# Order of the weight units in the feature-major products of an encoder trunk

## The chip, the cores and the metric

One core of one Trainium2 chip runs the whole program in one launch. The metric is device time in microseconds (us): the median of three runs of the kernel before is 2489.68 us (2489.42 to 2490.61).

## The reference

Two encoder layers over 256 tokens of width 2048, in float32. Layer 0 mixes with dilated-window attention (8 heads, three groups) and differential attention (4 heads), layer 1 with grouped-query attention (8 heads) and neighbourhood attention (8 heads). Every layer ends in a gated feed-forward part (FFN) of width 5632. Cut to what matters here:

```python
def conv_ffn(x, w_up, conv_w, conv_b, w_down):
    h = jnp.einsum("bsd,df->bsf", x, w_up)
    g, u = h[..., :D_FF], h[..., D_FF:]
    gp = jnp.pad(g, ((0, 0), (1, 1), (0, 0)))
    g = conv_w[0] * gp[:, :-2] + conv_w[1] * gp[:, 1:-1] + conv_w[2] * gp[:, 2:] + conv_b
    return jnp.einsum("bsf,fd->bsd", jax.nn.gelu(g) * u, w_down)

def reference(x, ...):
    for layer in range(DEPTH):
        y = rmsnorm(h, ln_mix[layer])
        mix = even_mixer(y, ...) if layer % 2 == 0 else odd_mixer(y, ...)
        h = h + mix
        h = h + conv_ffn(rmsnorm(h, ln_ffn[layer]), ...)
    return rmsnorm(h, ln_final)
```

Nearly all the arithmetic is products of the 256 token rows with weight matrices: the input projections of the attention, their output projections, the FFN's up (gate and value) and down.

## The kernel before, in words

**Precision.** Each float32 operand is split into a high part that TensorE takes as it is and a low part, the rest. A product is high times high, plus high times low, plus low times high, all summed in PSUM. For weights the high part `wh` is a cast by ScalarE (ACT, `split`, line 191) and the low part `wl` a subtraction by VectorE (DVE, line 192); each covers one unit of 128 x 1024 weights (`wunit`), which a DMA on the SP queue has brought. There are four buffers each for `wh` and `wl`, so a cast waits until TensorE has finished with the unit four before.

**Two kinds of product.** Token-major products (`gemm_a`, lines 152 to 154) have tokens on the output's partitions and only 512-column matmuls; they serve the FFN's down part, the output projections and some value projections. Feature-major products (`gemm_b`) have features on the output's partitions: they serve the queries and keys (48 + 16 + 16 of them) and the FFN's gate and value (176). One `gemm_b` sums over 2048 in two units of eight 128-blocks each. In `b_unit` each block has a 512-column matmul (line 124: `wh` times the activation's high and low parts side by side, 256 columns each) and a 256-column one (line 127: `wl` times the activation's high part, added onto the second half of the same PSUM bank). Per unit the eight of line 124 come first, then the eight of line 127. So a chain of `gemm_b` calls is eight wide, eight narrow, eight wide, eight narrow, and so on.

**Around it.** The result `gm` (four PSUM buffers) is taken out by `halves`: ACT copies the first half (line 181), DVE adds the second (line 182) and multiplies by the row factor (line 187). The small products of attention (transposes into `tp`, scores and values into `s`) are issued between two large products by a list of due times (`later`, `tick`, `flush`). A scheduler then puts each engine's instructions in order, by when it expects operands to be ready; where the first gate and value products of an FFN wait for the last transposed activations `yT`, it mixes their matmuls with the transposes (line 233).

Of the kernel before, what the change touches and what calls it, by code (L numbers as in the profile page):

```python
# [35 lines left out]
KT = D // P  # L36
# [21 lines left out]
def trunk_kernel(ctx: ExitStack, tc, a, out):  # L58
    nc = tc.nc
    V, S, G, T = nc.vector, nc.scalar, nc.gpsimd, nc.tensor  # L60
# [11 lines left out]
    def nm(s):  # L72
        uid[0] += 1
        return f"{s}_{uid[0]}"
# [27 lines left out]
    def tps(tag, bufs):  # L102
        return psum.tile([P, 512], F32, name=nm(tag), tag=tag, bufs=bufs)

    def wunit(src, parts=1):
        raw = wts.tile([P, UN], F32, name=nm("raw"), tag="raw", bufs=RAW)
        nc.sync.dma_start(raw, src)
        wh = wts.tile([P, UN], F32R, name=nm("wh"), tag="wh", bufs=4)
        wl = wts.tile([P, UN], F32R, name=nm("wl"), tag="wl", bufs=4)
        for i in range(parts):  # L110
            sl = slice(i * UN // parts, (i + 1) * UN // parts)
            split(wh[:, sl], wl[:, sl], raw[:, sl])
        return wh, wl

    def two(ap):
        return ap.rearrange("p (a b) -> p a b", a=2)

    def b_unit(ps, src, u, act):
        wh, wl = wunit(src[u])
        flat = ps.rearrange("p a b -> p (a b)")  # L120
        cols = [slice(k * P, (k + 1) * P) for k in range(8)]
        for k, sl in enumerate(cols):
            y = act[u * 8 + k]
            T.matmul(flat, wh[:, sl], y.rearrange("p a b -> p (a b)"), start=(u == 0 and k == 0), stop=False)  # L124
        for k, sl in enumerate(cols):
            y = act[u * 8 + k]
            T.matmul(ps[:, 1, :], wl[:, sl], y[:, 0, :], start=False, stop=(u * 8 + k == KT - 1))  # L127

    def gemm_b(src, act):

        ps = two(tps("gm", 4))
        for u in range(2):
            b_unit(ps, src, u, act)
        tick()
        return ps
# [20 lines left out]
    def gemm_a(src, act, nk, strided=False, hooks={}, first=1):  # L156

        ps = [tps("gm", 4), tps("gm", 4)]
        for u in range(nk // 2):
            if u in hooks:  # L160
                hooks[u]()
            a_unit(ps, src, u, act, nk, strided, parts=1 if u else first)
            if u % 2 == 1:
                tick()
        return ps
# [123 lines left out]
    def qk_tile(src, act, r, order, slot):  # L289
        t = halves(gemm_b(src, act), r, order)  # L290
        y = new_qk("qk", slot)
        split(y[:, 0, :], y[:, 1, :], t)
        return y
# [94 lines left out]
    ps = two(tps("tp", 2))  # L388
# [7 lines left out]
    ps = tps("s", 2)  # L396
# [4 lines left out]
    ps = tps("s", 2)  # L401
# [87 lines left out]
    for hh in range(2):  # L489
        vg = []  # L490
        for g in range(3):
            ps = v_ps.pop(0) if v_ps else gemm_a(a["eva_v"][hh * 3 + g], yT, KT, strided=(g > 0))
# [77 lines left out]
    for pair in range(2):  # L570
        vt = v_tiles(gemm_a(a["evb_v"][pair], yT, KT), rstd, range(20 - 4 * pair, 24 - 4 * pair))
        for hd in (2 * pair, 2 * pair + 1):
# [4 lines left out]
            for m in range(2):  # L577
                q = qk_tile(a["evb_qk"][hd * 4 + m], yT, Rq, rev, 2 * m)
                k = qk_tile(a["evb_qk"][hd * 4 + 2 + m], yT, R, None, 2 * m + 1)
# [5 lines left out]
    def ffn(layer, yT, gain, last=False):  # L585
        R = None
        res = None
        for half in range(2):
            prod = []
            for i in range(HALF_F):  # L590
                f = half * HALF_F + i
                if f == 0:
                    pg, pu = two(tps("gm", 4)), two(tps("gm", 4))
                    b_unit(pg, a["up"][layer, f, 0], 0, yT)
                    b_unit(pu, a["up"][layer, f, 1], 0, yT)
                    flush()
                    R = row_broadcast(row_factor())
                    b_unit(pg, a["up"][layer, f, 0], 1, yT)
                    b_unit(pu, a["up"][layer, f, 1], 1, yT)
                else:  # L600
                    pg = gemm_b(a["up"][layer, f, 0], yT)
                g = halves(pg, R)
                c = tmp.tile([P, SEQ], F32, name=nm("cv"), tag="cv")
                V.tensor_scalar(c, g, convw[:, layer, 1, f:f + 1], convb[:, layer, f:f + 1],
                                op0=ALU.mult, op1=ALU.add)
                V.scalar_tensor_tensor(c[:, 1:SEQ], g[:, 0:SEQ - 1], convw[:, layer, 0, f:f + 1],
                                       c[:, 1:SEQ], op0=ALU.mult, op1=ALU.add)
                V.scalar_tensor_tensor(c[:, 0:SEQ - 1], g[:, 1:SEQ], convw[:, layer, 2, f:f + 1],
                                       c[:, 0:SEQ - 1], op0=ALU.mult, op1=ALU.add)
                S.activation(c, c, AF.Gelu_apprx_tanh)  # L610
                if f:
                    pu = gemm_b(a["up"][layer, f, 1], yT)
                u = halves(pu, R)
                V.tensor_tensor(c, c, u, op=ALU.mult)
                y = new_act("prod", f % NACT)
                split(y[:, 0, :], y[:, 1, :], c)
                prod.append(y)
# [89 lines left out]
    ps = gemm_a(a["odc"][0], yT, KT, hooks={6: flush})  # L707
# [10 lines left out]
    for n in range(2):  # L718
        ps = gemm_a(a["odc"][1 + n], yT, KT)
# [6 lines left out]
    for hh in range(2):  # L726
        vt = v_tiles(gemm_a(a["od_v"][hh], yT, KT), rstd, ((18, 19, 20, 21), (16, 17, 22, 23))[hh])
        for hd in range(hh * 4, hh * 4 + 4):
            y = att.tile([P, 6, 64], F32, name=nm("nb"), tag="bias", bufs=2)
# [6 lines left out]
            k = qk_tile(a["od_qk"][hd * 2 + 1], yT, R, None, hd % 2 * 2 + 1)  # L736
# [157 lines left out]
```

## Time and profile before

| | |
|---|---|
| median of three runs | 2489.68 us |
| the profiled execution | 2489.95 us |
| its span, first to last instruction | 2488.2 us |
| TensorE (PE) busy | 99% of the span |
| weight loads (PEld) busy | 85% |
| VectorE (DVE) busy | 67% |
| ScalarE (ACT) busy | 49% |
| mean granted TensorE clock | 0.999 |

Rows of the timeline merge instructions of a kind that follow each other (x8). A matmul's duration in them is that of one matmul from its start to a modelled end, and consecutive matmuls overlap; what one costs in a chain is read from start to start.

### The profile page before, as it was taken

Reading aid. Unit: us, or ns where it says so; the run is one execution under the profiler, and the core shown is the slowest. Engines: PE = TensorE matmul, PEld = TensorE weight load, DVE = VectorE, ACT = ScalarE, POOL = GpSimd, SP = SyncE. Lnnn points to the kernel's source line nnn. Section 1 sums busy time; section 2 is a strip of 40 time slices with the busy share of each in tenths; the row PEclk is TensorE's granted clock in tenths of the full one; section 3 lists DMA queues with packets and bytes.
Section 4 is the critical chain, followed back from the end, with each engine's and each line's share of the span. In section 5 each row is a group of like instructions: output and inputs, shape, how many; then the busy total and the mean of one; then the engine's idle time right before and its main releaser. Section 6 shows DMA issues by size and latency. Waiting matters only on the chain.

```text
span 2488.2 us, 34307 instructions
## 1 busy us (share of the span) xinstructions
PE 2470.9 (99%) x13106; PEld 2122.7 (85%) x13106; DVE 1671.2 (67%) x2461; ACT 1227.6 (49%) x1853; POOL 35.9 (1%) x68
## 2 busy tenths in 40 slices
PE   8999999999999999999999999999999999999998
PEld 7888888888888888888888888888888888888887
DVE  5676577676577775577775568765777755777754
ACT  6454445465554443344444457545544443444443
POOL 1000000000000000000000000000000000000000
PEclk9999999999999999999999999999999999999999
DMA  8655555555555555555555555765555555555554
GB/s 296 197 175 176 185 178 179 173 176 156 187 189 190 187 188 192 195 188 190 190 186 187 187 185 170 173 176 178 187 188 190 189 187 194 194 187 188 191 189 144
DMA packets 129749, 463.86 MB, mean 186 GB/s; under 512 B 15188, under 2 KB 15220, under 8 KB 129584
## 3 DMA queue, kind: packets, MB, share of 16 engines
q1 hardware_dynamic: 126800, 455.17, 53.2%
q0 software_dynamic: 2784, 6.50, 2.4%
q8 instruction: 102, 1.67, 0.3%
q14 instruction: 63, 0.52, 0.1%
HBM read 459.44 MB, written 2.17 MB: 186 GB/s over the span
## 4 chain that ended last, share of the span: by engine, by line
PE 75%; DMA 0%; DVE 0%; ACT 0%; issue 0%; DVEq 0%; ACTq 0%
PE gm L124 28%; PE gm L127 15%; PE gm L153 10%; PE gm L152 10%; PE gm L154 10%; PE tp L233 0%; PE tp L326 0%; DMA nb<-in_rpb 0%; PE s L338 0%; PE s L337 0%; PE s L311 0%; PE s L309 0%; PE s L336 0%; PE s L310 0%; PE tp L668 0%; DVE wl L192 0%
## 5 line engine op out<-in xcount | busy, mean ns | idle before, releaser
L192 DVE TENSOR_TENSOR wl<-raw,wh 128x1024 fp32r<-128x1024 f32 (+1 forms) x857 | 1047.4, 1223 | 705.1 <-ACT wh L191 702.3
L191 ACT CAST wh<-raw 128x1024 fp32r<-128x1024 f32 (+1 forms) x857 | 898.7, 1049 | 1141.3 <-issue 498.7
L124 PE MATMUL gm<-yT,wh 128*128 128x512 f32 x4096 | 1029.1, 393 | 0.0
L124 PEld LDWEIGHTS gm<-yT,wh 128*128 128x128 f32 x4096 | 736.6, 189 | 132.5 <-DVE yT L196 0.7
L127 PEld LDWEIGHTS gm<-yT,wl 128*128 128x128 f32 x4096 | 558.7, 190 | 39.8
L127 PE MATMUL gm<-yT,wl 128*128 128x256 f32 x4096 | 571.2, 282 | 0.0
L152 PE MATMUL gm<-wh,prod 128*128 128x512 f32 x704 | 274.5, 390 | 0.0
L154 PE MATMUL gm<-wh,prod 128*128 128x512 f32 x704 | 274.3, 390 | 0.0
L153 PE MATMUL gm<-wl,prod 128*128 128x512 f32 x704 | 274.0, 389 | 0.0
L152 PE MATMUL gm<-wh,yT 128*128 128x512 f32 x416 | 164.9, 396 | 6.6 <-ACT wh L191 6.6
L153 PE MATMUL gm<-wl,yT 128*128 128x512 f32 x416 | 163.9, 394 | 0.3 <-DVE wl L192 0.3
L154 PE MATMUL gm<-wh,yT 128*128 128x512 f32 x416 | 163.5, 393 | 0.0
L154 PEld LDWEIGHTS gm<-wh,prod 128*128 128x128 f32 x704 | 132.2, 188 | 27.4
L152 PEld LDWEIGHTS gm<-wh,prod 128*128 128x128 f32 x704 | 132.2, 188 | 27.1
L153 PEld LDWEIGHTS gm<-wl,prod 128*128 128x128 f32 x704 | 132.2, 188 | 27.1
L182 DVE TENSOR_TENSOR t<-t,gm 128x256 f32<-128x256 f32 x256 | 105.9, 414 | 0.0
L153 PE MATMUL gm<-wl,mix 128*128 128x512 f32 x256 | 100.5, 393 | 1.1 <-DVE wl L192 1.1
L152 PE MATMUL gm<-wh,mix 128*128 128x512 f32 x256 | 101.0, 395 | 0.0
L154 PE MATMUL gm<-wh,mix 128*128 128x512 f32 x256 | 100.3, 393 | 0.0
L152 PEld LDWEIGHTS gm<-wh,yT 128*128 128x128 f32 x416 | 79.2, 190 | 22.7 <-ACT wh L191 6.6
L153 PEld LDWEIGHTS gm<-wl,yT 128*128 128x128 f32 x416 | 79.3, 191 | 17.0 <-DVE wl L192 1.6
L154 PEld LDWEIGHTS gm<-wh,yT 128*128 128x128 f32 x416 | 79.1, 190 | 16.5
(206 smaller groups left out, 1506.4 us busy)
## 6 DMA issues: line engine op xcount, KB each, us to landing
raw<-in_up SPq DMA_DIRECT2D x352, 512.0 KB, 3.3
raw<-in_down SPq DMA_DIRECT2D x176, 512.0 KB, 3.2
raw<-in_eva_qk SPq DMA_DIRECT2D x96, 512.0 KB, 3.2
raw<-in_eva_v SPq DMA_DIRECT2D x48, 512.0 KB, 3.7
raw<-in_evb_qk SPq DMA_DIRECT2D x32, 512.0 KB, 3.3
raw<-in_ev_out SPq DMA_DIRECT2D x32, 512.0 KB, 3.5
raw<-in_od_qk SPq DMA_DIRECT2D x32, 512.0 KB, 3.3
raw<-in_od_out SPq DMA_DIRECT2D x32, 512.0 KB, 3.3
```

Source lines behind the costliest of these rows:

```text
L124: T.matmul(flat, wh[:, sl], y.rearrange("p a b -> p (a b)"), start=(u == 0 and k == 0), stop=False)
L127: T.matmul(ps[:, 1, :], wl[:, sl], y[:, 0, :], start=False, stop=(u * 8 + k == KT - 1))
L152: T.matmul(ps[t], ah, wh[:, sl], start=(kt == 0), stop=False)
L153: T.matmul(ps[t], ah, wl[:, sl], start=False, stop=False)
L154: T.matmul(ps[t], al, wh[:, sl], start=False, stop=(kt == nk - 1))
L182: V.tensor_tensor(t0, t0, ps[:, 1, :], op=ALU.add)
L191: S.copy(dst_h, src)
L192: V.tensor_tensor(dst_l, src, dst_h.bitcast(F32), op=ALU.subtract)
```

## The change

In `b_unit` the first unit (u = 0) keeps its order, and the second unit issues its eight 256-column matmuls ahead of its eight 512-column ones. The flag that closes the sum moves from the last narrow matmul to the last wide one. Number, shape and operands of the matmuls stay the same. Lines behind the edit stand three lower in the changed file; there the wide matmul is line 127 and the narrow one line 130.

```diff
--- before.py
+++ after.py
@@ -119,12 +119,15 @@
         wh, wl = wunit(src[u])
         flat = ps.rearrange("p a b -> p (a b)")
         cols = [slice(k * P, (k + 1) * P) for k in range(8)]
-        for k, sl in enumerate(cols):
+        high = [(True, k, sl) for k, sl in enumerate(cols)]
+        low = [(False, k, sl) for k, sl in enumerate(cols)]
+        for hi, k, sl in high + low if u == 0 else low + high:
             y = act[u * 8 + k]
-            T.matmul(flat, wh[:, sl], y.rearrange("p a b -> p (a b)"), start=(u == 0 and k == 0), stop=False)
-        for k, sl in enumerate(cols):
-            y = act[u * 8 + k]
-            T.matmul(ps[:, 1, :], wl[:, sl], y[:, 0, :], start=False, stop=(u * 8 + k == KT - 1))
+            if hi:
+                T.matmul(flat, wh[:, sl], y.rearrange("p a b -> p (a b)"), start=(u == 0 and k == 0),
+                         stop=(u * 8 + k == KT - 1))
+            else:
+                T.matmul(ps[:, 1, :], wl[:, sl], y[:, 0, :], start=False, stop=False)
 
     def gemm_b(src, act):
```

On TensorE, in a gate product in mid FFN (`gm_7013`; `wh_7016` and `wl_7017` are its first unit's weights, `wh_7038` and `wl_7039` its second's, `gm_7068` the product behind it), the order before is:

```order
L127 MATMUL gm_7013<-yT_6139,wl_7017 128x256
L124 MATMUL gm_7013<-yT_6297,wh_7038 128x512 [waits Activation_49]
L124 MATMUL gm_7013<-yT_6302,wh_7038 128x512
...
L124 MATMUL gm_7013<-yT_6495,wh_7038 128x512
L127 MATMUL gm_7013<-yT_6297,wl_7039 128x256 [waits DVE_49]
...
L127 MATMUL gm_7013<-yT_6495,wl_7039 128x256
L124 MATMUL gm_7068<-yT_6101,wh_7071 128x512 [waits Activation_49]
L124 MATMUL gm_7068<-yT_6106,wh_7071 128x512
```

In the change the same place on TensorE reads:

```order
L130 MATMUL gm_7013<-yT_6139,wl_7017 128x256
L130 MATMUL gm_7013<-yT_6297,wl_7039 128x256 [waits DVE_49]
L130 MATMUL gm_7013<-yT_6302,wl_7039 128x256
...
L130 MATMUL gm_7013<-yT_6495,wl_7039 128x256
L127 MATMUL gm_7013<-yT_6297,wh_7038 128x512 [waits Activation_49]
...
L127 MATMUL gm_7013<-yT_6495,wh_7038 128x512
L127 MATMUL gm_7068<-yT_6101,wh_7071 128x512 [waits Activation_49]
L127 MATMUL gm_7068<-yT_6106,wh_7071 128x512
```

The eight narrow rows of the second unit now stand right behind those of the first, and its eight wide rows right ahead of those of the next product. The wait for `wl_7039` (a DVE result) comes eight wide matmuls earlier than before.

On ACT, in the same part (casts `wh` of coming units, the copy `t` out of the products `gm_7013` and `gm_7068`, the GELU `cv`), the order before is:

```order
L181 COPY t_1376_7058<-gm_7013 128x256 [waits PE_49]
L191 CAST wh_7180<-raw_7178 128x1024 [waits DMAHW7_49,PE_49,Activation_49]
L191 CAST wh_7202<-raw_7200 128x1024 [waits DMAHW0_49,PE_49,Activation_49]
L610 ACTIVATE cv_7063<-cv_7063 128x256 [waits DVE_49]
L181 COPY t_1386_7113<-gm_7068 128x256 [waits PE_49]
L191 CAST wh_7234<-raw_7232 128x1024 [waits DMAHW1_49,PE_49,Activation_49]
L191 CAST prod_7119<-cv_7063 128x256 [waits DVE_49]
L191 CAST wh_7256<-raw_7254 128x1024 [waits DMAHW2_49,PE_49,Activation_49]
```

In the change the same place on ACT reads:

```order
L184 COPY t_1376_7058<-gm_7013 128x256 [waits PE_49]
L194 CAST wh_7147<-raw_7145 128x1024 [waits DMAHW6_49,Activation_49]
L194 CAST wh_7180<-raw_7178 128x1024 [waits DMAHW7_49,PE_49,Activation_49]
L613 ACTIVATE cv_7063<-cv_7063 128x256 [waits DVE_49]
L184 COPY t_1386_7113<-gm_7068 128x256 [waits PE_49]
L194 CAST wh_7202<-raw_7200 128x1024 [waits DMAHW0_49,Activation_49]
L194 CAST prod_7119<-cv_7063 128x256 [waits DVE_49]
L194 CAST wh_7234<-raw_7232 128x1024 [waits DMAHW1_49,PE_49,Activation_49]
```

The cast of `wh_7202`, which waits for a second unit's buffer, has moved behind the GELU and the copy out of `gm_7068`.

On TensorE at the first FFN's start (transposes `tp` of the last activations; `gm_6430` the first gate, `gm_6431` the first value product, `gm_6577` the next gate), ahead of the second-last pair of transposes, the order before is:

```order
L233 MATMUL tp_6487<-ident,h 128x128 [waits PE_49]
L233 MATMUL tp_6487<-ident,h 128x128
L124 MATMUL gm_6430<-yT_6297,wh_6516 128x512 [waits Activation_49]
L124 MATMUL gm_6430<-yT_6302,wh_6516 128x512
...
L124 MATMUL gm_6431<-yT_6297,wh_6538 128x512 [waits Activation_49]
L124 MATMUL gm_6431<-yT_6302,wh_6538 128x512
L124 MATMUL gm_6431<-yT_6308,wh_6538 128x512
L233 MATMUL tp_6476<-ident,h 128x128 [waits DVE_49]
L233 MATMUL tp_6476<-ident,h 128x128
```

In the change that place on TensorE reads:

```order
L236 MATMUL tp_6487<-ident,h 128x128 [waits PE_49]
L236 MATMUL tp_6487<-ident,h 128x128
L130 MATMUL gm_6430<-yT_6297,wl_6517 128x256
L130 MATMUL gm_6430<-yT_6302,wl_6517 128x256
...
L130 MATMUL gm_6430<-yT_6479,wl_6517 128x256 [waits Activation_49]
L130 MATMUL gm_6431<-yT_6297,wl_6539 128x256 [waits DVE_49]
...
L130 MATMUL gm_6431<-yT_6479,wl_6539 128x256
L127 MATMUL gm_6577<-yT_6101,wh_6580 128x512
L236 MATMUL tp_6476<-ident,h 128x128 [waits DVE_49]
L236 MATMUL tp_6476<-ident,h 128x128
```

Where seven wide matmuls stood ahead of the next pair of transposes, there are now ten narrow ones and one wide one.

## Rows read from the trace of the kernel before

**Rows 1.** The page: busy us (share) by engine.
```profile
PE 2470.9 (99%) x13106; PEld 2122.7 (85%) x13106; DVE 1671.2 (67%) x2461; ACT 1227.6 (49%) x1853; POOL 35.9 (1%) x68
```

**Rows 2.** Waits of PE: engine, line waited for: us in total, times, longest.
```profile
PE gm L152 <- ACT wh L191: 6.6, 1, 6.6
PE gm L153 <- DVE wl L192: 1.3, 2, 1.1
PE tp L326 <- DVE sc L533: 0.8, 1, 0.8
```

**Rows 3.** Groups by line on PE: xcount | busy us, mean ns | idle before.
```profile
L124 PE MATMUL gm<-yT,wh 128*128 128x512 f32 x4096 | 1029.1, 393 | 0.0
L127 PE MATMUL gm<-yT,wl 128*128 128x256 f32 x4096 | 571.2, 282 | 0.0
```

**Rows 4.** Timeline of PE, chain of feature-major products: start, us, engine, line, xcount.
```profile
1281.37 2.00 PE L124 MATMUL gm<-yT,wh 128*128 128x512 f32 x8
...
1284.17 2.00 PE L124 MATMUL gm<-yT,wh 128*128 128x512 f32 x8
1286.01 1.11 PE L127 MATMUL gm<-yT,wl 128*128 128x256 f32 x8
1286.96 2.00 PE L124 MATMUL gm<-yT,wh 128*128 128x512 f32 x8
...
1297.18 1.11 PE L127 MATMUL gm<-yT,wl 128*128 128x256 f32 x8
1298.13 2.00 PE L124 MATMUL gm<-yT,wh 128*128 128x512 f32 x8
```

**Rows 5.** Timeline of PE: wide run behind a token-major product; inside another one.
```profile
1055.14 1.98 PE L124 MATMUL gm<-yT,wh 128*128 128x512 f32 x8
1056.96 1.11 PE L127 MATMUL gm<-yT,wl 128*128 128x256 f32 x8
...
1303.22 0.39 PE L153 MATMUL gm<-wl,prod 128*128 128x512 f32 x1
...
1311.61 0.39 PE L154 MATMUL gm<-wh,prod 128*128 128x512 f32 x1
```

**Rows 6.** Timeline of PE, where twelve 256-column value products follow a narrow run.
```profile
545.23 1.11 PE L127 MATMUL gm<-yT,wl 128*128 128x256 f32 x8
546.18 0.28 PE L548 MATMUL s<-v,pt 128*128 128x256 f32 x1
...
547.62 2.00 PE L124 MATMUL gm<-yT,wh 128*128 128x512 f32 x8
549.46 1.12 PE L127 MATMUL gm<-yT,wl 128*128 128x256 f32 x8
```

**Rows 7.** Timeline of all engines at the first FFN's start (PEld: weight loads).
```profile
694.07 1.87 PE L124 MATMUL gm<-yT,wh 128*128 128x512 f32 x7
...
695.18 0.48 DVE L196 SCALAR_TENSOR_TENSOR yT<-tp,ln,yT 128x256 fp32r<-128x256 f32 x1
...
695.71 0.20 PEld L233 LDWEIGHTS tp<-ident,h 128*128 128x128 f32 x2 [0.21 <-DVE yT L196]
695.77 0.38 PE L233 MATMUL tp<-ident,h 128*128 128x128 f32 x2
...
695.91 1.40 PE L124 MATMUL gm<-yT,wh 128*128 128x512 f32 x5
...
697.24 0.20 PEld L247 LDWEIGHTS tp<-ident,rb 128*128 128x128 f32 x2 [0.36 <-DVE yT L196]
```

**Rows 8.** Timeline of ACT and DVE in the chain of rows 4.
```profile
1286.25 1.05 ACT L191 CAST wh<-raw 128x1024 fp32r<-128x1024 f32 x1 [1.47 <-issue]
...
1287.44 1.22 DVE L192 TENSOR_TENSOR wl<-raw,wh 128x1024 fp32r<-128x1024 f32 x1
```

**Rows 9.** Waits of DVE.
```profile
DVE nb L699 <- DMA nb<-in_rpb: 29.4, 8, 5.1
```

**Rows 10.** Timeline of DVE at the end of layer 0's attention.
```profile
580.70 1.22 DVE L192 TENSOR_TENSOR wl<-raw,wh 128x1024 fp32r<-128x1024 f32 x1
...
587.33 0.56 DVE L699 TENSOR_TENSOR nb<-nb,colmask 128x384 f32<-128x384 f32 x1 [5.08 <-DMA nb<-in_rpb]
...
590.13 1.22 DVE L192 TENSOR_TENSOR wl<-raw,wh 128x1024 fp32r<-128x1024 f32 x1
```

**Rows 11.** Stretch of FFN: us, PE, PEld, DVE, ACT, POOL busy (xcount), PEclk, DMA.
```profile
703.00:934.00 231.00, 231.00 (x1325) 203.30 (x1324) 175.69 (x275) 112.17 (x167) 0.00 (x0) 1.00 0.56 191
```

## The prediction

> **What bounds the kernel now.** I read the page's busy shares first, then TensorE's waits, then its groups by line, then its timeline from start to start. TensorE (PE) is busy for 99% of the span [rows 1], and in all of it three waits stand out, 8.7 us together, 6.6 us of which lie at the program's start before any feature-major product [rows 2]. Through a long stretch of the FFN it is busy for 231.00 of 231.00 us at a granted clock of 1.00, the upper of its two levels, 2.4 GHz [rows 11]. So the time is the sum of what the matmuls cost in their chain, and ACT and DVE matter only where they would make TensorE wait. The reader is to see that busy time does not give that cost: 4096 matmuls of 393 ns and 4096 of 282 ns [rows 3] would be 2765 us, more than the span. They overlap, so I go by distances between starts.
>
> **What a matmul costs, by its place in the chain.** Inside a token-major product, 37 wide (512-column) matmuls lie between the starts 1303.22 and 1311.61 [rows 5]: 8.39/37 = 226.8 ns each, so eight cost 1.814. The wide run of eight that follows such a product takes 1056.96 - 1055.14 = 1.82 [rows 5], the same. Twelve narrow (256-column) ones in a row behind eight other narrow ones take 547.62 - 546.18 = 1.44 [rows 6], 120 ns each, so eight cost 0.960. Eight wide and eight narrow should then take 2.774 us. In the chain of feature-major products six such rounds take 1298.13 - 1281.37 = 16.76 [rows 4], 2.793 a round, 19 ns more. The timeline shows where: the wide run behind a narrow one takes 1286.01 - 1284.17 = 1.84, some 26 ns above its steady cost, and the narrow run behind a wide one 1286.96 - 1286.01 = 0.95, some 7 ns below it [rows 4]. Each passage from narrow to wide and back costs 19 ns net.
>
> Does that price depend on how long the narrow run was? Behind twenty narrow matmuls (eight of line 127, twelve value products) the wide run takes 549.46 - 547.62 = 1.84 [rows 6], as behind eight. So doubling the narrow run should not raise it.
>
> **The change part by part.** No matmul, load, cast or DMA is added or removed. Per product there were two passages from narrow to wide: inside it, and from its last narrow run to the next product. Now the second narrow run joins the first and the second wide run joins what comes next, so one is left. There are 4096/16 = 256 products [rows 3]. The passage goes only where wide matmuls follow at once. Where attention's small products stand behind, as in [rows 6], the new chain is wide, narrow, wide, small, wide, and nothing is won. Counted over the scheduled order of TensorE, narrow-to-wide passages go from 519 to 314: 205 fewer. Gain: 205 x 0.019 = 3.9 us. Its bounds are 0 and 256 x 0.019 = 4.9.
>
> *The start of each FFN.* Here the change costs something. The first products wait for the last activations, and the scheduler fills in matmuls that are ready. Before, seven wide ones (694.07 to 695.77) covered the time until DVE had emptied the transposes' buffer at 695.18 + 0.48 = 695.66; the load of the next transposes waits for exactly that [rows 7]. Now ten narrow and one wide stand there, 10 x 0.120 + 0.227 = 1.43, over at 695.50, so TensorE stands still for about 0.27. The next pair is released by DVE at 697.24 [rows 7]; by then the new order (two transposes 0.14, four wide, two narrow) reaches 695.77 + 0.14 + 0.91 + 0.24 = 697.06, another 0.18. Both gaps were covered by wide matmuls before. I take 0.5 per start with the pair behind, two starts, 1.0 us; bounds 0 and 2.
>
> *Weights asked for earlier.* The second unit's narrow run needs `wl` 1.84 us sooner, and its wide run gives `wh` back 0.95 us later, so the cast for the unit four further on, and the subtraction behind it, start 0.95 later. The cast at 1286.25 gives a `wl` that is ready at 1287.44 + 1.22 = 1288.66 [rows 8]; four units after the buffer's release, it is first used at 1297.18 [rows 4]: 8.5 us to spare. Of that 1.84 + 0.95 goes; 5.7 stay. Behind the cast that now waits longer on ACT stand, in the order shown, a cast of activations and the next unit's cast, and DVE's `wl` waits for these; all lie inside the same 5.7. I cost it at nothing. If the cover were gone it would cost up to 1.84 per product.
>
> *The waits left.* The two waits in mid-program, 0.8 for attention scores and 1.3 for `wl` of a token-major product [rows 2], lie where the chain of DVE ends last, outside the edited loop. I leave them as they are; bounds are 2.1 either way. The copy out of `gm` starts after the last matmul as before: a last wide one starts 227 ns ahead of the next matmul and lasts 0.39, a last narrow one 120 ns ahead and lasts 0.28, so both end about 0.16 behind the next start.
>
> **Sum.** 2489.95 (the profiled execution: span 2488.2 and 1.75 around it) - 3.9 + 1.0 = 2487.05. That execution lies 0.27 above the median of the runs, so I forecast a median of 2486.8, 0.12% below 2489.68. What a measurement here can tell from no change is about 0.2%, 5.0 us.
>
> **A rule against it.** The starts in [rows 4] put a price on the order, 19 ns a round. The Trainium skill, page "TensorE: Matmul & The Clock Gate", section "Back-to-back issue gap", gives the isolated gap as N/2.4 ns plus 2.5, by the column count N alone. By that rule order is worth nothing and the sum would be its second rival below; the trace does not agree, since the same eight wide matmuls take 1.82 or 1.84 by what stands ahead.
>
> **Rivals.**
> 1. *The price grows with the run.* If the 26 ns were a backlog that eight narrow matmuls build and sixteen double, one passage would cost 52 and save 7 once: 45 ns where two cost 38. Then 205 x 0.007 = +1.4, with the FFN starts +2.4: 2492.1. For it: weight loads are busy 85% of the span [rows 1], so loads may lag in narrow runs. Against it: the unchanged 1.84 behind twenty [rows 6].
> 2. *Only the columns count.* The 19 ns go elsewhere (to another place of the round) and nothing is won: 2489.7, or 2490.7 with the FFN starts. For it: 19 of 2793 ns is near what two decimals show. Against it: six rounds add up to 0.115 us.
> 3. *Slower: `wl` of the second unit comes late.* DVE works in order, and eight times its queue stands behind a DMA for `nb`, 29.4 us together [rows 9]; once two `wl` are 590.13 - 580.70 = 9.4 us apart [rows 10]. If at all eight places TensorE now had to wait for the 1.84 by which it asks sooner: 8 x 1.84 = 14.7, 2501.5. It decides once less than 2.8 us is to spare there before. Against it: no wait for `wl` in the whole program is longer than 1.1 us [rows 2], that hole included.
> 4. *Faster.* All 256 products win and both mid-program waits go, with no loss at the FFN starts: 2489.7 - 4.9 - 2.1 = 2482.7. For it: any shift in DVE's order can remove a wait. Against it: the small products do stand behind many gemms.
>
> **Chances.** Forecast 0.70 (2484.9 to 2488.8), rival 1 0.06, rival 2 0.10, rival 3 0.06, rival 4 0.08. The range leaves out rivals 1 and 3 and most of 4: 2484.3 to 2490.2. Faster by over 0.2% (below 2484.7) is rival 4 and the forecast's edge, 0.12. Slower by over 0.2% (above 2494.7) is rival 3, 0.05. The rest, 0.83, is no change that can be told.
>
> **What would show it.** In the changed profile the timeline of an FFN should show sixteen narrow and sixteen wide: narrow 16 x 0.120 - 0.007 = 1.91, wide 16 x 0.2268 + 0.026 = 3.65, a product 5.57 where two rounds took 5.59. A wide run of 3.68 or more speaks for rival 1; 5.59 for rival 2. A wait of TensorE for DVE `wl` by the narrow line speaks for rival 3. At the FFN's start gaps of 0.2 to 0.3 before the transposes should stand. I am wrong if the gain exceeds 5 us, or if the time rises at all.

## The result, and the profile after

The changed kernel takes 2492.78 us (median of 22 runs, 2490.69 to 2495.93), the kernel before 2489.81 (22 runs, 2489.08 to 2491.31): a ratio of 1.0012, 95% interval 1.0007 to 1.0018. It is slower by 3 us, less than the 5 us that I took for the bound of what can be told, but 22 runs of each tell them apart. The forecast was 2486.8 and the range ended at 2490.2: both the size and the direction were wrong. The profiled execution took 2493.40 us.

The first view is the page, here of the changed kernel: busy shares, two DMA queues, the chain that ended last by engine and by line, and the FFN's weight loads with their median time to landing.

```profile
PE 2469.0 (99%) x13106; PEld 2123.8 (85%) x13106; DVE 1656.4 (66%) x2461; ACT 1240.4 (50%) x1853; POOL 35.8 (1%) x68
...
q1 hardware_dynamic: 126800, 455.17, 57.8%
q0 software_dynamic: 2784, 6.50, 2.7%
...
PE 71%; DMA 2%; DVE 2%; issue 0%; POOL 0%; ACT 0%; DVEq 0%; POOLq 0%; ACTq 0%
...
raw<-in_up SPq DMA_DIRECT2D x352, 512.0 KB, 3.8
```

The same lines of the kernel before (its busy line is in [rows 1]):

```profile
q1 hardware_dynamic: 126800, 455.17, 53.2%
q0 software_dynamic: 2784, 6.50, 2.4%
...
PE 75%; DMA 0%; DVE 0%; ACT 0%; issue 0%; DVEq 0%; ACTq 0%
...
raw<-in_up SPq DMA_DIRECT2D x352, 512.0 KB, 3.3
```

The busy shares tell nothing: TensorE was 99% busy and still is. The chain that ended last tells more: it now runs for 2% of the span through DMAs and 2% through DVE; before, both were 0%. The same 126800 packets and 455.17 MB of weights also hold the DMA engines for 57.8% of the span instead of 53.2%, an FFN load taking 3.8 us where it took 3.3. Little can be built on that difference: kernels of the experiments below with the old order in the FFN (e2, e3, e6, e8, e9) show 56.1 to 56.8% and 3.4 to 3.9 us.

Second view: what TensorE waits for in the changed kernel (us in total, times, longest), the answer to [rows 2].

```profile
PE gm L155 <- ACT wh L194: 6.4, 1, 6.4
PE gm L156 <- DVE wl L195: 3.3, 3, 1.4
PE s L340 <- DVE pt L195: 2.6, 3, 1.4
PE tp L329 <- DVE sc L536: 1.8, 1, 1.8
```

Behind the wait at the program's start there were 2.1 us in three waits (one of them, 0.3, still in the first 12 us); now there are 7.7 in seven, all for DVE, none by the narrow line 130. DVE in turn stands longer where it stood before [rows 9]:

```profile
DVE nb L702 <- DMA nb<-in_rpb: 41.0, 8, 7.4
```

To see where the 3.4 us between the two spans arose, I compared the start of the same matmul in both profiled executions:

| TensorE at the same matmul | before | after | later by |
|---|---|---|---|
| scores near the end of layer 0's attention | 576.72 | 576.48 | -0.24 |
| transposes behind them (L326, now L329) | 589.54 | 590.32 | +0.78 |
| first transposes of the first FFN | 693.71 | 694.23 | +0.52 |
| a token-major product in layer 1's attention | 1580.04 | 1578.96 | -1.08 |
| value products (L337, now L340) | 1609.25 | 1611.64 | +2.39 |
| the same line, later | 1645.24 | 1647.65 | +2.41 |
| the same line, later | 1658.28 | 1663.43 | +5.15 |
| last matmul | 2479.32 | 2482.75 | +3.43 |

TensorE gains steadily wherever it waits for nothing, and loses in three short stretches: 0.78 + 0.24 = 1.02, 2.39 + 1.08 = 3.47 and 5.15 - 2.41 = 2.74, together 7.2. All the rest is 3.43 - 7.23 = -3.8. The listed waits grew by less, 7.7 - 2.1 = 5.6; in part because a listed wait begins at the modelled end of the matmul before: at 1594.51, seen below, TensorE starts 1594.51 - 1593.10 - 0.23 = 1.18 us late for a listed 1.02.

What happens in the second stretch is seen in DVE's timeline of the changed kernel:

```profile
1585.00 1.23 DVE L195 TENSOR_TENSOR wl<-raw,wh 128x1024 fp32r<-128x1024 f32 x1
1592.77 0.56 DVE L702 TENSOR_TENSOR nb<-nb,colmask 128x384 f32<-128x384 f32 x1 [6.54 <-DMA nb<-in_rpb]
1593.24 1.22 DVE L195 TENSOR_TENSOR wl<-raw,wh 128x1024 fp32r<-128x1024 f32 x1
...
1596.98 0.69 DVE L195 TENSOR_TENSOR pt<-tp,pt 128x512 fp32r<-128x512 f32 x1
1597.58 0.68 DVE L705 TENSOR_TENSOR scc<-s,nb 128x512 f32<-128x512 f32 x1
```

The same rows of DVE in the kernel before:

```profile
1588.89 0.56 DVE L699 TENSOR_TENSOR nb<-nb,colmask 128x384 f32<-128x384 f32 x1 [3.92 <-DMA nb<-in_rpb]
1589.37 1.22 DVE L192 TENSOR_TENSOR wl<-raw,wh 128x1024 fp32r<-128x1024 f32 x1
...
1593.10 0.68 DVE L192 TENSOR_TENSOR pt<-tp,pt 128x512 fp32r<-128x512 f32 x1
```

DVE adds the column mask to the bias tile `nb` of an attention head. In its order that instruction stands ahead of weights and of the softmax of an earlier head; until the bias lands, all of these stand too. Now the bias lands 3.9 us later. TensorE in the changed kernel:

```profile
1593.10 0.39 PE L155 MATMUL gm<-wh,yT 128*128 128x512 f32 x1
1594.51 0.50 PE L156 MATMUL gm<-wl,yT 128*128 128x512 f32 x1 [1.02 <-DVE wl L195]
...
1597.16 0.28 PE L339 MATMUL s<-pt,v 128*128 128x256 f32 x1
1597.72 0.39 PE L340 MATMUL s<-pt,v 128*128 128x256 f32 x1 [0.29 <-DVE pt L195]
```

The `wl` that a token-major product needs is there at 1593.24 + 1.22 = 1594.46. TensorE asks at 1593.10 + 0.23 = 1593.33, stands, and stands again at the values for `pt`. Of the 3.9 us before DVE goes on, 0.8 come from a later issue of the load (GpSimd at 1581.58, before at 1580.78) and 3.1 from a longer load: 1592.77 - 1581.58 = 11.2 us from issue to the mask, before 8.1.

The chain that ended last, in this stretch of the changed kernel, shows how one delay is handed on:

```profile
1581.58 0.45 POOL nb L735
1582.22 10.45 DMA nb<-in_rpb
1593.24 1.22 DVE wl L195
...
1597.06 0.60 DVE pt L195
1597.66 0.61 DVE scc L705
1598.27 0.28 issue
1598.55 0.47 POOL nb L735
1599.19 8.69 DMA nb<-in_rpb
```

It is a loop. There are two bias buffers; the next load is issued when DVE has read an older bias into scores (`scc`), and that DVE instruction stands behind the mask of the bias that is being loaded. So a load, DVE's queue behind it, and the next load follow one another. This turn, from the load of head 4 to that of head 5, took 1598.55 - 1581.58 = 17.0 us; before, 1594.68 - 1580.78 = 13.9 (the two issues on GpSimd). The other short turns grew by 1.3 us in sum: 15.8, 12.7 and 14.4, where they were 14.2, 13.3 and 14.1. Between 1575 and 1670 us, 46.9% of the changed kernel's chain is the DMA of `nb`; before, the chain there ran through TensorE's matmuls alone. Whether the loop itself adds to the loss, beyond each single delay, is not shown: in e9 below the waits stand although the chain in that stretch runs mostly through TensorE.

### The profile page after: what moved, and what is told of

It reads as the page before. It is cut to its first block, busy times and chain, and to the rows that moved or that the text cites. A ratio compares the mean times of both kernels' runs of the same rounds, so it can differ in the third digit from the quotient of the medians.

```text
span 2491.6 us, 34288 instructions
## 1 busy us (share of the span) xinstructions
PE 2469.0 (99%) x13106; PEld 2123.8 (85%) x13106; DVE 1656.4 (66%) x2461; ACT 1240.4 (50%) x1853; POOL 35.8 (1%) x68
## 3 DMA queue, kind: packets, MB, share of 16 engines
q1 hardware_dynamic: 126800, 455.17, 57.8%
## 4 chain that ended last, share of the span: by engine, by line
PE 71%; DMA 2%; DVE 2%; issue 0%; POOL 0%; ACT 0%; DVEq 0%; POOLq 0%; ACTq 0%
PE gm L127 27%; PE gm L130 14%; PE gm L157 10%; PE gm L156 10%; PE gm L155 10%; DMA nb<-in_rpb 2%; DVE wl L195 1%; PE tp L236 0%; DVE scc L705 0%; PE tp L329 0%; DVE pt L195 0%; POOL nb L735 0%; DVE nb L702 0%; PE s L340 0%; PE tp L671 0%
## 5 line engine op out<-in xcount | busy, mean ns | idle before, releaser
L127 PE MATMUL gm<-yT,wh 128*128 128x512 f32 x4096 | 991.1, 391 | 0.0
L127 PEld LDWEIGHTS gm<-yT,wh 128*128 128x128 f32 x4096 | 748.9, 188 | 142.7
L130 PEld LDWEIGHTS gm<-yT,wl 128*128 128x128 f32 x4096 | 525.9, 191 | 21.6 <-ACT yT L198 1.2
L130 PE MATMUL gm<-yT,wl 128*128 128x256 f32 x4096 | 534.0, 283 | 0.0
L184 ACT COPY t<-gm 128x256 f32<-128x256 f32 x256 | 95.3, 372 | 374.5 <-PE gm L127 374.4
L613 ACT ACTIVATE cv<-cv 128x256 f32<-128x256 f32 x88 | 36.8, 418 | 166.1 <-DVE cv L611 166.1
L155 PEld LDWEIGHTS gm<-wh,yT 128*128 128x128 f32 x416 | 79.5, 191 | 22.5 <-ACT wh L194 6.4
```

Source lines behind the costliest of these rows:

```text
L155: T.matmul(ps[t], ah, wh[:, sl], start=(kt == 0), stop=False)
L184: S.copy(t0, ps[:, 0, :])
```

## The experiments

**The two kinds of product apart.** A flag chooses the new order for the FFN's 176 products alone (e1), or for the 80 query and key products of attention alone (e2).

```diff
-        for hi, k, sl in high + low if u == 0 else low + high:
+        for hi, k, sl in low + high if u and joined else high + low:
```

> The new order for the 176 FFN products alone; the 80 query and key products of attention keep the old order. All theories agree on the FFN: 175 passages fewer at 19 ns, 3.3 us gained, no loss at the two FFN starts (the changed profile showed none). Theory A (TensorE is late in attention because DVE stands behind a load of nb) and theory B (because wl of the second unit is asked for 1.84 us sooner and cast later) both put the whole loss of 7 us into the attention stretches, so 2486.5 and the waits of before, about 2 us in mid-program. If the loss came from the FFN's bunched weight loads (theory C, two loads 1.5 us apart, then 4.05 us nothing), the waits at 588 and at 1590 to 1665 us would stand here too: 2492.

Measured: 2486.32 us (2485.83 to 2487.25) beside 2489.77, ratio 0.9986 (0.9977 to 0.9995): 3.45 us faster.

> The new order for the 80 query and key products of attention alone, the FFN as before. Theories A and B: the passages removed in attention give 0.5 to 0.6 us, the waits added cost 7: 2496, with waits at 588 and 1590 to 1665 us as in the changed kernel. Theory C (bunched loads in the FFN): no added waits, 2489.3.

Measured: 2495.43 us (2494.90 to 2497.65), ratio 1.0024 (1.0014 to 1.0034). TensorE's waits in it are those of the changed kernel within 0.1 us. So the FFN wins what the passages promise (175 of them at 19 ns are 3.3 us), and all of the loss comes from the new order in attention. The two add up to 5.66 - 3.45 = +2.2 us, beside the +3.0 of the whole change.

**The mask on GpSimd.** Both kernels with the mask's addition moved off DVE, so that DVE's queue no longer stands behind the load (this standing is called the hold below); e3 is the kernel before, e4 the changed one.

```diff
-        V.tensor_tensor(y, y, colmask.unsqueeze(1).to_broadcast([P, 6, 64]), op=ALU.add)
+        G.tensor_tensor(y, y, colmask.unsqueeze(1).to_broadcast([P, 6, 64]), op=ALU.add)
```

> The kernel before, with the addition of the column mask to nb (one instruction per neighbourhood head, 8 in all) moved from DVE to POOL, so that DVE no longer stands behind the load of nb. Theory A: DVE's 29 us behind nb vanish, and with them the wait of TensorE for scores at 588 us, perhaps the 1.1 us for wl behind it: 2488 to 2489. Theory B: no change beyond 0.3 us, 2489.8.

Measured: 2487.24 us, ratio 0.9989 (0.998 to 0.9998).

> The changed kernel with the same move of the mask to POOL. Theory A: the waits for pt, wl and scores at 588 and 1590 to 1665 us vanish, the gain of the passages stays: 3.9 us below the kernel before with the mask on POOL, 2484.5 to 2485. Theory B: wl is still asked for 1.84 us sooner, the waits stay: 2491 to 2493.

Measured: 2483.52 us, ratio 0.9974 (0.9964 to 0.9985). TensorE's waits, whole answer, in e4:

```profile
PE gm L155 <- ACT wh L194: 6.6, 1, 6.6
```

Only the program's start is left. Both came out some 1 us below the times expected of theory A. Without the hold the new order is worth 2487.24 - 2483.52 = 3.7 us, and the same edit gives back 2492.78 - 2483.52 = 9.3 us of the changed kernel but 2.6 us of the kernel before. That closes the account: the hold costs 9.3 - 2.6 = 6.7 us more than before, the order saves 3.7, and the change measured +3.0.

**The mask added late.** The same on DVE: the mask is added to the scores, behind the bias, instead of to the bias tile (e5 changed, e6 before). DVE does a little more work, but waits for no load.

```diff
-        V.tensor_tensor(y, y, colmask.unsqueeze(1).to_broadcast([P, 6, 64]), op=ALU.add)
...
         V.tensor_tensor(sc, ps, bias_view(y.rearrange("p a b -> p (a b)"), P), op=ALU.add)
+        rows = sc.rearrange("p t (r c) -> p (t r) c", c=64)
+        V.tensor_tensor(rows, rows, colmask.unsqueeze(1).to_broadcast([P, 8, 64]), op=ALU.add)
```

> The changed kernel with the column mask added on DVE still, but to the scores after nb has been added to them (8 x 64 columns), so that DVE touches nb only when the scores are there, 25 to 40 us after its load. Theory A (DVE standing behind the load of nb) gives the same as with the mask on POOL: 2483.5, no wait of DVE for a DMA of nb, no mid-program wait of TensorE. If the gain of the POOL version came from taking work off DVE (8 x 0.56 us) and not from the standing, this keeps the loss: 2491 to 2493.

Measured: 2483.39 us (2482.60 to 2484.21), ratio 0.9974 (0.9963 to 0.9984). TensorE's waits in it:

```profile
PE gm L155 <- ACT wh L194: 6.4, 1, 6.4
```

> The kernel before with the same late mask. Theory A: 2487.2 as with the mask on POOL; the difference to the changed kernel with the late mask is the price of the passages, 3.7 to 3.9 us. Otherwise 2489.8.

Measured: 2487.15 us, ratio 0.9989 (0.9981 to 0.9998). The difference of the pair is 3.76 us. It is not GpSimd that helps but that nothing of DVE's queue stands behind the load. Version e5 lies 6.4 us below the kernel before in the same runs (2489.82); it, e4 and e10 below are within 0.2 us of each other.

**The load of the bias by itself.** If a longer load alone does it, the old matmul order must lose too. In e9, the kernel before gets a third small load behind the bias of heads 0, 4 and 7; in e10, the changed kernel reads its bias from stretches of 1536 bytes instead of pieces of 256 (as many bytes, other values).

```diff
+            if hd in (0, 4, 7):
+                G.dma_start(y[0:64, 0:1, :], bass.AP(tensor=rpb.tensor, offset=rpb.offset + hd * 465 + 31 * 4 - 48,
+                                                     ap=[[1, 64], [31, 1], [1, 64]]))
```

> The kernel before, in which three of the eight loads of nb (neighbourhood heads 0, 4 and 7, those that took 1.6 to 3.1 us longer in the changed kernel) are made longer by a small third load of the same values behind the two. Matmul order, casts and weight loads stay as before. Theory A1 (the longer loads of nb are enough to make TensorE wait): the three loads take 10 to 12 us, DVE stands 36 to 42 us behind nb, TensorE waits at 588 and between 1585 and 1670 us for scores, wl or pt, 2 to 7 us in all beyond the 2.1 of before: 2492 to 2496. Theory A2 (the waits need DVE's new order): under 1 us more, at most 2490.8.

Measured: 2496.47 us (2493.15 to 2499.86), ratio 1.0025 (1.0015 to 1.0035). TensorE's waits, and DVE's for the bias, in e9:

```profile
PE gm L152 <- ACT wh L191: 6.3, 1, 6.3
PE tp L326 <- DVE sc L533: 3.0, 1, 3.0
PE s L337 <- DVE pt L192: 1.9, 2, 1.2
PE gm L153 <- DVE wl L192: 1.6, 3, 0.9
PE s L336 <- ACT pt L191: 1.2, 1, 1.2
...
DVE nb L699 <- DMA nb<-in_rpb: 39.9, 8, 7.5
```

With not one matmul moved, nor an instruction of ACT, and DVE's order the same but for a few instructions, waits of the same kind appear. From issue to mask the three loads took 10.2, 11.6 and 12.8 us. The median is above the 2492 to 2496 that theory A1 gave. In the profiled execution, 7.8 us above that of the kernel before, some 1.4 us of this are no wait: behind the stall of 3.0 us TensorE's granted clock is 0.57 from 593 to 596 us, which is its lower level, 1.2 GHz, for most of that time, and seven 512-column matmuls start 0.43 us apart instead of 0.23.

```diff
-                    tensor=rpb.tensor, offset=rpb.offset + hd * 465 + 31 * (4 + il) - 48,
-                    ap=[[1, 64], [31, 6], [1, 64]]))
+                    tensor=rpb.tensor, offset=rpb.offset + hd * 400 + 31 * il,
+                    ap=[[1, 64], [64, 6], [1, 64]]))
```

> The changed kernel with nb read from 64 contiguous stretches of 1536 bytes per half instead of 384 of 256 bytes (the same bytes moved, other values, so it computes other numbers). The loads of nb should take some 4 to 6 us instead of 7 to 12, and nothing else changes. Theory A: DVE stands under 20 us behind nb, the waits of TensorE in attention go but for 0 to 1 us: 2483.5 to 2485. If DVE's place in the order and not the load's length makes the waits, they stay: 2490 or more.

Measured: 2483.55 us, ratio 0.9973 (0.9963 to 0.9983). In e10:

```profile
PE gm L155 <- ACT wh L194: 6.2, 1, 6.2
PE gm L156 <- DVE wl L195: 0.8, 2, 0.5
...
DVE nb L702 <- DMA nb<-in_rpb: 6.5, 5, 2.0
```

The 0.8 us stand in the program's first 18 us. The mask stays in DVE's queue, the load takes 3.4 to 4.0 us, and 9.2 us come back. In e4, e5 and e10 the matmuls stand in the changed kernel's order, so `wl` of the second unit is asked for as early as there, and nothing waits for it in the feature-major products.

**Why the load is longer.** One theory was that the new order makes the weight loads come in pairs, which hold the DMA engines beside the bias. In e7 the second unit of the query and key products of the eight heads with a bias is not loaded; the first unit's weights stand in for it.

```diff
+        if again:
+            raw = last_raw[0]
...
-        wh, wl = wunit(src[u])
+        wh, wl = wunit(src[u], again=half and u == 1)
```

> The changed kernel, but the second unit of the 16 query and key products of the neighbourhood heads is not loaded: the first unit's raw weights are cast a second time, so it computes other numbers and moves 8 MB less there. This asks why DVE stands longer behind nb in the changed kernel (41 us where 29). Theory A1 (weight loads now come in pairs 1.1 to 1.5 us apart and the loads of nb share the DMA engines with them, so these take up to 11.7 us where 9.1): with half the weight traffic the five later loads of nb fall to 7 to 8 us, and the waits of TensorE at 1590 to 1665 us, 6.4 us, go or fall below 1.5: 2486 to 2487.5. Theory A2 (only DVE's new order, which reaches scores and masks at other times): loads of nb may shorten but the waits stay above 4 us: 2490 or more.

Measured: 2488.02 us (2486.90 to 2488.92), ratio 0.9993 (0.9984 to 1.0002), 0.5 us above what theory A1 gave. TensorE's waits, and DVE's for the bias, in e7:

```profile
PE tp L335 <- DVE sc L542: 1.7, 1, 1.7
PE gm L162 <- DVE wl L201: 0.9, 1, 0.9
...
DVE nb L708 <- DMA nb<-in_rpb: 34.7, 8, 6.5
```

TensorE no longer waits between 1590 and 1665 us, but of the five loads that were to shrink to 7 to 8 us, those of heads 4 and 7 did not. The issue times of the weight loads on the SP queue tell why. The table has, for each bias load, the time from issue to mask in us, and in brackets how long after its issue a weight load was issued while it was under way:

| head | before | changed | e7 |
|---|---|---|---|
| 0 | 8.1 (2.7) | 9.7 (2.8, 3.9) | 9.6 (2.8, 3.9) |
| 1 | 7.9 (2.9) | 7.7 (2.9) | 7.7 (2.9) |
| 2 | 8.7 (2.5, 5.3) | 7.6 (1.8) | 6.6 (none) |
| 3 | 8.3 (2.5, 5.3) | 7.2 (1.8) | 7.3 (1.8) |
| 4 | 8.1 (3.2) | 11.2 (2.5, 4.7) | 10.1 (2.5, 4.7) |
| 5 | 8.5 (2.1, 4.8) | 9.4 (1.8, 4.0) | 7.6 (4.0) |
| 6 | 7.6 (2.6) | 8.8 (2.2, 3.3) | 7.3 (2.3) |
| 7 | 9.1 (2.2, 4.6) | 11.7 (2.5, 3.6) | 10.8 (2.5, 3.6) |

From before to changed, the load grows where a second weight load came in (heads 0, 4, 6) or where two came closer together (5, 7), shrinks where one went (2, 3) and stays where nothing moved (1). In e7 it shrinks by 1.0 to 1.8 us where one went (2, 5, 6); at heads 4 and 7 two weight loads still stand beside the bias (at head 7 those of the output projection), and it shrinks by 1.1 and 0.9. So e7 bears the theory out in the main: the loads that lost a neighbour are back at 6.6 to 7.6 us, the two that lost none are still at 10.1 and 10.8. It also shows that a load of 10 us need not make TensorE wait: at heads 4 and 7 DVE stood for 5.5 and 6.5 us, and TensorE did not.

**The passage by itself.** In e8, the kernel before with the mask on GpSimd does four wide and four narrow in turn: 512 more passages.

```diff
+        for part in (range(4), range(4, 8)):
+            for k in part:
+                T.matmul(flat, wh[:, cols[k]], y.rearrange("p a b -> p (a b)"), start=(u == 0 and k == 0), stop=False)
+            for k in part:
+                T.matmul(ps[:, 1, :], wl[:, cols[k]], y[:, 0, :], start=False, stop=(u * 8 + k == KT - 1))
```

> The kernel before with the mask on POOL, and each unit issued as four wide, four narrow, four wide, four narrow: two passages more per product, 512 in all, with no move between units. If every passage from narrow to wide costs 19 ns net as measured, 512 x 0.019 = 9.7 us more than 2487.2: 2496.9. If the surcharge is spread over the first five wide matmuls and a run of four takes only its first four (6 + 9 + 1 + 6 ns) less 7, 15 ns: 2494.9. If it is no price of the passage but of the round of sixteen, 2487.2.

Measured: 2493.03 us (2491.92 to 2493.36), 5.8 us above e3; the two theories with a price of the passage had expected 9.7 and 7.7, the third none. Its TensorE in mid FFN:

```profile
1283.41 1.09 PE L125 MATMUL gm<-yT,wh 128*128 128x512 f32 x4
1284.34 0.64 PE L128 MATMUL gm<-yT,wl 128*128 128x256 f32 x4
...
1289.02 1.09 PE L125 MATMUL gm<-yT,wh 128*128 128x512 f32 x4
```

Four rounds take 1289.02 - 1283.41 = 5.61, 1.4025 each, where four wide and four narrow at their steady cost are 4 x 0.2268 + 4 x 0.120 = 1.387: 15.5 ns a passage. Two such replace one of 19, which is 12 ns by 512, or 6.1 us. A short wide run pays less than a full one, and the expectation had left out that the passages that were there already get cheaper too.

## Why the prediction was wrong, point by point

**Price of the passage: right.** TensorE in an FFN of the changed kernel, the answer to [rows 4]:

```profile
1281.30 3.82 PE L127 MATMUL gm<-yT,wh 128*128 128x512 f32 x16
1284.96 2.08 PE L130 MATMUL gm<-yT,wl 128*128 128x256 f32 x16
1286.87 3.82 PE L127 MATMUL gm<-yT,wh 128*128 128x512 f32 x16
```

Wide 3.66, narrow 1.91, a product 5.57, against 3.65, 1.91 and 5.57 foretold. Rivals 1 (a wide run of 3.68 or more) and 2 (5.59) fall. The pairs without the hold give 3.7 and 3.8 us for the 3.9 of the sum. So order has a price. The isolated gap by the column count alone, as the Trainium skill's page "TensorE: Matmul & The Clock Gate", section "Back-to-back issue gap", has it, would give 0 for both pairs, and it does not describe this chain.

**Starts of the FFN: priced about 0.5 too high each.** The first one in the changed kernel, the answer to [rows 7]:

```profile
694.23 0.60 PE L236 MATMUL tp<-ident,h 128*128 128x128 f32 x4
694.59 1.57 PE L130 MATMUL gm<-yT,wl 128*128 128x256 f32 x10
696.00 0.39 PE L127 MATMUL gm<-yT,wh 128*128 128x512 f32 x1
696.24 0.44 PE L236 MATMUL tp<-ident,h 128*128 128x128 f32 x2
...
703.24 2.08 PE L130 MATMUL gm<-yT,wl 128*128 128x256 f32 x16
```

The gap is there: 696.24 - 694.59 = 1.65 for work of 1.43. But I had set it against none before, and [rows 7] show otherwise: seven wide took 695.77 - 694.07 = 1.70 for work of 1.59, and five took 697.24 - 695.91 = 1.33 for 1.13; both rows of weight loads carry a wait for DVE. From the first transposes over 24 wide and 24 narrow matmuls it is 9.88 us before (693.71 to 703.59) and 9.97 after (to 703.24 plus eight narrow, 0.96). So it costs 0.1, not 0.5. The second start, counted the same way, takes 10.05 us before (1752.45 to 1762.50) and 10.00 after (1757.66 to 1766.82 plus seven narrow, 0.84): nothing.

**The waits left: the step that failed.** The prediction put them as lying "outside the edited loop. I leave them as they are; bounds are 2.1 either way". That term was held to be 0, at most 2.1 either way; it measured +6.7 by the medians (9.3 us of hold in the changed kernel, 2.6 before) and +7.2 in the stretches of the profiled execution. The runs show: DVE in order behind the load of the bias (e4 and e5: without it TensorE has no wait left in mid-program), and the load's length as what decides, since lengthening it brings such waits with the old matmul order (e9) and shortening it takes them away with the new one (e10). [Rows 9 and 10] held it: a queue that stands 29.4 us behind a DMA, and a chain that already ended last at 0.8 and 1.3 us. I asked there only whether `wl` of the edited loop would be late, not what would happen to the 0.8 and 1.3 if the DMA landed later.

**Weights asked for earlier: the cost was nothing, the consequence was not.** TensorE never waits by the narrow line, as said. But the argument was about casts, from a steady FFN, and left out the DMAs that the casts set free. The buffers are now released in pairs, and the weight loads with them: in mid FFN (800 to 840 us) their issues lie 1.5 and 4.05 us apart in turn, where they lay mostly 2.7 to 2.9 apart. In the stretch of [rows 11] (the last three: granted clock, DMA share, GB/s) the changed kernel reads:

```profile
703.00:934.00 231.00, 231.00 (x1333) 204.32 (x1332) 173.24 (x275) 115.03 (x168) 0.00 (x0) 1.00 0.62 190
```

DMA engines are busy for 0.62 instead of 0.56 while moving 190 GB/s instead of 191; but the same stretch reads 0.58 to 0.61 in e2, e3, e6, e8 and e9, which keep the old order in the FFN, so at most part of this is the pairs. In any case the FFN covers it: e1 has these pairs too and only gains. What the bias loads meet are the weight loads of attention, in the table under e7.

**Rival 3 had the place, not the mechanism.** It named DVE behind the eight loads of `nb`, but priced it by the 1.84 us of an earlier need for `wl`, and got 2501.5. What decides is when the load lands.

**What stays open.** That the bias loads take longer with the new order is measured: issue to mask 66.3 us over the eight heads before, 73.3 after, with 7.2 us more at heads 0, 4 and 7 and the others cancelling out. It is no result of the hold, since with the mask on GpSimd those three take 9.4, 9.7 and 10.9 us in e4 and 8.5, 8.3 and 8.7 in e3. It comes with the new order in attention: 9.6, 10.5 and 11.6 in e2, 8.6, 8.2 and 9.7 in e1. The table under e7 ties the length to the weight loads issued beside the bias, and e7 shows it where it took one away. A run with loads in pairs under the old order was not made. What the two kinds of load share is not shown either, nor how much longer a load may get before TensorE waits.

## What to carry to other kernels

Before reordering work on a busy engine, look for an in-order queue that stands behind a DMA whose result is needed much later; where the busy engine already waits behind that queue, as it did here for 0.8 and 1.1 us, such a load costs time as soon as it grows. A wait of 0.8 us is then no small term but a sign that the slack there is gone. When an edit changes when buffers are released, follow the loads this triggers into the stages that do not belong to the edit.

## What the runs showed of the hardware that was not expected

A 512-column matmul behind 256-column ones is dearer over its first five: in the changed kernel's run of sixteen at 1281.30 the first five starts lie 234, 235, 229, 232 and 231 ns apart, the ten behind them 226 or 227. The five pay 27 ns above the steady 226.8, the first four 23; less the 7 that the narrow run saves, that fits the 15.5 ns a passage for runs of four (e8) and the 19 for runs of eight.

A bias load of two times 96 KB in 256-byte pieces took 7.2 to 11.7 us from issue to mask beside the weight loads in the changed kernel, and 3.4 to 4.0 us in 1536-byte stretches (e10).

Behind a stall of TensorE of 3.0 us (e9) the granted clock from 593 to 596 us was 0.57; behind the stall of 1.8 us at the same place in the changed kernel it was 1.00 (590.4 to 594 us).
